# The MLP's features of groups 1 to 3 as seven products of half-size blocks

## The chip, the cores and the metric

The kernel runs on one core of one Trainium2 chip. Its metric is the device time of one execution in microseconds (us); a median over runs is given. Five engines work side by side, each through its own instructions in order: TensorE (PE in the profile; its weight loads are PEld), VectorE (DVE), ScalarE (ACT), GpSimd (POOL) and SyncE (SP, which here only issues DMAs).

## The reference, cut to what matters

A bidirectional encoder trunk of two layers on 512 tokens of width 1024. Layer 0 mixes tokens by a gated DeltaNet, layer 1 by GLA; behind each mixer stands a squared-ReLU MLP with a hidden width of 4096. The change lies in the MLP, which runs twice:

```python
def _sq_relu_mlp(h, w1, w2):
    a = jax.nn.relu(jnp.matmul(h, w1))       # w1: 1024 x 4096
    return jnp.matmul(a * a, w2)             # w2: 4096 x 1024
...
x = _layernorm(DEEPNORM_ALPHA * x + _sq_relu_mlp(x, mlp_w1[i], mlp_w2[i]), ln2_g[i], ln2_b[i])
```

Everything is float32.

## The kernel before

**Arithmetic.** Each float32 operand of a product is split into a high part (ACT casts it to fp32r, `split`, line 98) and the rest (VectorE subtracts, line 99). `mm3` (lines 117 to 119) then makes three matmuls: high by high, high by low, low by high. "A split" below is the pair of instructions of lines 98 and 99; on VectorE both of its inputs lie in SBUF.

**Groups.** `mlp` cuts the hidden width into G = 4 groups of GF = 8 features of 128 columns. A feature (`feature`, `proj_cm`) is W1's 128 columns times all of x, transposed (`xth`, `xtl`: 8 blocks of 128 rows, 512 tokens): 8 blocks x 3 matmuls, 24 matmuls of 512 columns into a PSUM bank `pj`; ACT then takes ReLU and square into `h` (`act`).

**W2 of groups 0 to 2.** `second` multiplies a group's activations by its rows of W2 as 2 x 2 blocks, in seven products instead of eight (Strassen's scheme in Winograd's form). The blocks of W2 are loaded by DMAs that POOL issues (`load_part`, line 371) into tiles `w2r`; the sums of blocks that the scheme needs are made by `plus` (line 390): DMAs that add one tile to another, issued by POOL. The differences of activations are made by VectorE (`s1`, `a21`, `a11`, `a12`). A product has 24 matmuls of 512 columns, into banks X, Y, Z; VectorE adds the result to the residual `xt` (`add`, lines 406 and 408).

**Order.** Group 0's first four features run in two halves of 256 tokens (`proj_halves`), the rest plainly. Then each product of group gi is followed by one feature of group gi + 1 (`nxt`): seven products, eight features. Group 3's W2 (`last`) is multiplied plainly, by token tiles (banks `pl`), with a LayerNorm behind each tile. The order on PE and POOL is that of the text (`in_order`); ACT and VectorE are ordered by the scheduler of the framework, when the kernel is compiled. Tiles come from rings by tag: `wst` (W1 as loaded, 3), `wh`/`wl` (3), `w2r` (10), `w2h`/`w2l` (3), `ah`/`al` (2).

In the second MLP, `affine` applies the previous LayerNorm's scale and shift to x on VectorE in group 0 (lines 201 and 202).

Of the kernel before, what the change touches and what calls it, by code (L numbers as in the profile page):

```python
# [28 lines left out]
class Ctx:  # L29
# [153 lines left out]
    def whiten(self, xs):  # L183

        nc = self.nc
        st = self.small.tile([P, 2, 6], F32, name="bst", tag="bst1", bufs=4)
# [48 lines left out]
    def layernorm(self, z, out, par, last=False, split=1):  # L235
# [3 lines left out]
        st = self.small.tile([P, 2 * split, 6], F32, name="bst", tag=f"bst{split}", bufs=4 // split)  # L239
# [91 lines left out]
def mlp(c, w1, w2, g, b, left, before=None, out=None):  # L331
# [13 lines left out]
    with c.banks(pj=2, X=2, Y=2, Z=2), tc.tile_pool(name="mlp", bufs=2) as pool:  # L345
        par = None
        acts = []
# [3 lines left out]
        RING = {"ah": ("ah", "al", 2), "w2": ("w2h", "w2l", 3), "raw": ("w2r", "w2r", 10)}  # L351
# [9 lines left out]
        def raw():  # L361
            return pool.tile([P, 2, 512], F32, name="w2r", tag="w2r", bufs=10)
# [24 lines left out]
        def plus(a, b):  # L387

            for q in range(2):
                nc.gpsimd.dma_start(blocks[a + (q,)], blocks[b + (q,)], accum_op=ALU.add)  # L390

# [3 lines left out]
        def feature(gi, f, h):  # L395
            return act(c.proj_cm(w1, (gi * GF + f) * P, "pj"), h[f // HF][:, f % HF, :])
# [12 lines left out]

        def quarters(h):  # L410
            return [h[j][:, :, HT * i:HT * i + HT] for i in range(2) for j in range(2)]

        def second(gi, h, a, nxt):

            a11, a12, a21, a22 = quarters(h)
# [4 lines left out]
            def product(bk, a, i, new, by_tile=False):  # L420

                if i not in parts:
                    split(i)
                ws = parts.pop(i)
                order = [(q, j) for j in range(2) for q in range(2)] if by_tile else [(q, j) for q in range(2) for j in range(2)]
                for q, j in order:
                    wh, wl = ws[q]
                    sl = slice(j * P, (j + 1) * P)
                    for k in (2 * q, 2 * q + 1):
                        c.mm3(bk[j], a[0][:, k, sl], a[1][:, k, sl], wh[:, k % 2, :], wl[:, k % 2, :],  # L430
                              new and k == 0, k == HF - 1, skip_group_check=True)

            def fetch(i, j):
                if gi + 2 < G:
                    load(gi + 1, i, j, acts[-1])

            X, Y = banks("X"), banks("Y")
            product(X, a, 1, True)
            for j in range(2):
                add(j, 0, X[j])  # L440
            nxt()
            Z = banks("Z")
            product(Z, pair(a12), 2, True)
            s1 = pool.tile([P, HF, HT], F32, name="s1", tag="s1", bufs=1)
            V.tensor_tensor(s1, a22, a21, ALU.subtract)
            V.tensor_tensor(a21, a11, a21, ALU.subtract)
# [1129 lines left out]
```

## Time and profile before

| | |
|---|---|
| Median of 3 runs (lowest, highest) | 1369.61 us (1368.17, 1369.61) |
| The profiled execution: its time, its span | 1368.45 us, 1366.5 us |
| Mean TensorE clock granted | 0.996 of full speed |
| Busy in the span: PE, DVE, ACT, POOL | 98%, 70%, 51%, 10% |
| First MLP: first product of W2, first matmul of group 3's W2 | 475.56 us, 721.8 us |
| Mean DMA rate | 104 GB/s |

How to read it: the span goes from the first to the last instruction; the time of an execution also holds what lies around it. Times of instructions are microseconds from the span's start, then the duration. Matmuls overlap, so that what one costs in a row of them is the distance from start to start, not its duration. In rows of groups, "x" is the count, then come the busy time and the mean length in ns, and after the bar the idle time of the engine before these instructions and what ended it. The idle time of an engine that is not the bottleneck costs nothing.

### The profile page before, as it was taken

To read this page: it belongs to the slowest core of one execution; us is meant where nothing else is said; L and a number is where in the kernel's file an instruction comes from. 1 tells how busy PE (TensorE), PEld (TensorE's weight loads), DVE (VectorE), ACT (ScalarE), POOL (GpSimd) and SP (SyncE) were. 2 spreads that over 40 slices of the span, in tenths; PEclk is the share of its full clock that TensorE was granted. 3 is DMA by queue.
4 is the path that set the end of the run, shared out by engine and by line. 5 is a ranking of instruction groups with operands and counts; after the bars stand their busy time and mean duration, and the time that the engine had idled before them with its cause. 6 is when DMAs were issued, how large, how long until landed. Compare 5 with 4: busy or idle time off the path is not lost.

```text
span 1366.5 us, 20078 instructions
## 1 busy us (share of the span) xinstructions
PE 1345.9 (98%) x7925; PEld 1114.8 (82%) x7925; DVE 950.7 (70%) x1502; ACT 692.7 (51%) x1293; POOL 138.0 (10%) x216
## 2 busy tenths in 40 slices
PE   7999999999999999999999999999999999999997
PEld 6778787877788888888888988888879888888886
DVE  5798988888867375655655677977773956556555
ACT  3667566565734554444443354654466544444430
POOL 6000040000002111201000000000001212120000
PEclk9999999999999999999999999999999999999999
DMA  6311121211234676747522222221224957566121
GB/s 166 88 48 47 38 57 47 63 48 32 79 96 121 190 167 196 172 124 185 108 93 59 62 84 77 62 63 62 90 65 150 228 148 214 139 191 133 50 81 55
DMA packets 148261, 142.62 MB, mean 104 GB/s; under 512 B 9583, under 2 KB 124391, under 8 KB 148167
## 3 DMA queue, kind: packets, MB, share of 16 engines
q1 hardware_dynamic: 132224, 86.45, 22.2%
q0 software_dynamic: 15232, 54.55, 15.9%
q8 instruction: 62, 1.02, 0.3%
q10 hardware_dynamic: 711, 0.34, 0.1%
q14 instruction: 32, 0.26, 0.1%
HBM read 114.06 MB, written 2.10 MB: 85 GB/s over the span
## 4 chain that ended last, share of the span: by engine, by line
PE 89%; ACT 5%; DVE 2%; POOL 1%; issue 1%; DMA 1%; SPq 0%; DVEq 0%; POOLq 0%; ACTq 0%
PE pj L118 8%; PE pj L117 8%; PE pj L119 8%; PE pjv L118 3%; PE pjv L119 3%; PE pjv L117 3%; PE pX L119 2%; PE pX L117 2%; PE pX L118 2%; PE pl L117 2%; PE pl L119 2%; PE pl L118 2%; PE scp L817 2%; PE op L1506 2%; PE lv L1382 2%; PE pZ L119 2%
## 5 line engine op out<-in xcount | busy, mean ns | idle before, releaser
L99 DVE TENSOR_TENSOR wl<-wst,wh 128x1024 fp32r<-128x1024 f32 x137 | 169.3, 1237 | 186.8 <-ACT wh L98 186.8
L98 ACT CAST wh<-wst 128x1024 fp32r<-128x1024 f32 x137 | 144.0, 1051 | 250.1 <-PE pj L118 182.1
L118 PE MATMUL pj<-xtl,wh 128*128 128x512 f32 (+1 forms) x544 | 202.1, 371 | 0.3 <-DVE xtl L168 0.3
L117 PE MATMUL pj<-xth,wh 128*128 128x512 f32 (+1 forms) x544 | 202.1, 371 | 0.3 <-ACT xth L167 0.3
L119 PE MATMUL pj<-xth,wl 128*128 128x512 f32 (+1 forms) x544 | 201.7, 371 | 0.0
L99 DVE TENSOR_TENSOR w2l<-w2r,w2h 128x1024 fp32r<-128x1024 f32 x84 | 102.5, 1221 | 62.8 <-ACT w2h L98 62.7
L118 PEld LDWEIGHTS pj<-xtl,wh 128*128 128x128 f32 x544 | 102.5, 188 | 18.5 <-DVE xtl L168 0.8
L117 PEld LDWEIGHTS pj<-xth,wh 128*128 128x128 f32 x544 | 102.4, 188 | 18.4 <-ACT xth L167 0.5
L119 PEld LDWEIGHTS pj<-xth,wl 128*128 128x128 f32 x544 | 102.5, 188 | 17.7
L98 ACT CAST w2h<-w2r 128x1024 fp32r<-128x1024 f32 x84 | 88.3, 1052 | 44.9 <-PE pZ L119 14.4
L98 ACT CAST ah<-h 128x1024 fp32r<-128x1024 f32 x40 | 42.1, 1052 | 41.6 <-PE pX L118 16.9
L371 POOL DMA_DIRECT2D w2r<-in_mlp_w x48 | 35.0, 731 | 276.0 <-ACT h L358 178.5
L390 POOL DMA_DIRECT2D w2r<-w2r x48 | 41.4, 926 | 178.9 <-DVE w2l L99 123.5
L117 PE MATMUL pX<-w2h,ah 128*128 128x512 f32 x144 | 56.3, 391 | 0.0
L119 PE MATMUL pX<-w2h,al 128*128 128x512 f32 x144 | 56.3, 391 | 0.0
L118 PE MATMUL pX<-w2l,ah 128*128 128x512 f32 x144 | 56.0, 389 | 0.0
L99 DVE TENSOR_TENSOR al<-h,ah 128x1024 fp32r<-128x1024 f32 x40 | 48.9, 1222 | 9.6 <-ACT ah L98 8.1
L117 PE MATMUL pjv<-wh,xth 128*128 128x512 f32 x128 | 54.7, 427 | 0.0
L119 PE MATMUL pjv<-wh,xtl 128*128 128x512 f32 x128 | 50.2, 392 | 0.0
L118 PE MATMUL pjv<-wl,xth 128*128 128x512 f32 x128 | 49.9, 390 | 0.0
L214 ACT ACTIVATE rsy<-rsv 128x1 f32<-128x1 f32 (+1 forms) x28 | 5.7, 203 | 77.9 <-DVE rsv L211 77.2
L117 PE MATMUL pjk<-xth,wh 128*128 128x512 f32 (+1 forms) x112 | 42.3, 378 | 0.3 <-ACT wh L98 0.3
(440 smaller groups left out, 3460.2 us busy)
## 6 DMA issues: line engine op xcount, KB each, us to landing
wst<-in_mlp_w SPq DMA_DIRECT2D x80, 512.0 KB, 4.3
w2r<-in_mlp_w POOLq DMA_DIRECT2D x48, 512.0 KB, 5.7
w2r<-w2r POOLq DMA_DIRECT2D x48, 512.0 KB, 5.8
wst<-in_a_w_in SPq DMA_DIRECT2D x32, 512.0 KB, 4.1
wst<-in_b_w_in SPq DMA_DIRECT2D x32, 256.0 KB, 3.1
wst<-in_a_w_out SPq DMA_DIRECT2D x8, 512.0 KB, 3.9
wst<-in_b_w_in SPq DMA_DIRECT2D x8, 512.0 KB, 3.8
wst<-in_b_w_out SPq DMA_DIRECT2D x8, 512.0 KB, 3.6
```

The costliest lines, as they stand in the source:

```text
L98: nc.scalar.copy(hi, src)
L99: nc.vector.tensor_tensor(lo, src, hi.bitcast(F32), ALU.subtract)
L117: mm(ps, ah, bh, start=start, stop=False, **kw)
L118: mm(ps, ah, bl, start=False, stop=False, **kw)
L119: mm(ps, al, bh, start=False, stop=stop, **kw)
L214: nc.scalar.activation(y, v, AF.Ln, scale=-2.0)
L371: ins = nc.gpsimd.dma_start(t, w2[r:r + 2 * P, 512 * j:512 * j + 512].rearrange("(k p) n -> p k n", p=P))
L390: nc.gpsimd.dma_start(blocks[a + (q,)], blocks[b + (q,)], accum_op=ALU.add)
L817: T.matmul(ps[:, n, :], kh[:, sl], qh[:, sl], start=True, stop=True)
L1382: T.matmul(ps[:, u, :, :], lhs[:, u, :], cols(rhs, u, s, i), start=True, stop=True)
L1506: T.matmul(op[:, n, :], l, r, start=i == 0, stop=i == len(mm) - 1)
```

## The change

Pairs of features of groups 1 to 3 (12 pairs an MLP) become 2 x 2 block products: x in halves of 512 rows and of 256 tokens, W1 in halves of 512 rows and two features. Seven products of 4 blocks x 3 matmuls of 256 columns replace 2 x 24 matmuls of 512. The combinations of x are made once (`combos`, VectorE, in group 0, into tiles `t0` to `t5`, the last one in place of x's block). The sums of W1 blocks are GpSimd additions on the loaded tiles (`total`, four of 512 columns a pair), and the sums of W2 blocks become GpSimd additions too (`sums`, eight of 1024 columns a group) in place of DMAs. A pair has 3.5 splits of 1024 columns where it had two. The seven results are put together by ACT (copies out of PSUM) and VectorE (`pairs`).

W1's pairs (`pairs`) and W2's products (`seconds`, cut into units of six matmuls) are two generators; the main loop draws a step of one and a unit of the other in turn, seven of each for a pair. The order on ACT is now the written one, too, in this stretch. A product's splits are issued one product ahead, its additions to `xt` one unit behind. Five splits of group 3's W2 and activations are drawn into the last two products (`last`, now a generator with homes chosen by hand). Half of `affine` goes to GpSimd. The ring of `w2r` has 8 tiles instead of 10, the pool `small` 3 instead of 4.

The diff, cut:

```diff
-    def proj_cm(self, w, c0, tag, n=P, name="pj"):
-
-        wh, wl = self.wcols(w, c0, n)
+    def proj_cm(self, w, c0, tag, n=P, name="pj", parts=None):
+
+        wh, wl = parts or self.wcols(w, c0, n)
...
-            self.nc.vector.tensor_tensor(x, x, par[q], ALU.mult)
-            self.nc.vector.tensor_tensor(x, x, par[2 + q], ALU.add)
+            eng = self.nc.vector if q else self.nc.gpsimd
+            eng.tensor_tensor(x, x, par[q], ALU.mult)
+            eng.tensor_tensor(x, x, par[2 + q], ALU.add)
...
-        def split(i):
-
-            i_, j_ = {1: (0, 0), 2: (1, 0), 3: (1, 1), 4: (1, 0), 5: (0, 0), 6: (0, 0), 7: (0, 1)}[i]
-            parts[i] = [c.split(blocks[i_, j_, q], [P, 2, 512], pool=ring("w2")) for q in range(2)]
-
-            if i == 1:
-                plus((0, 0), (0, 1))
-                plus((0, 1), (1, 1))
-            elif i == 5:
-                plus((0, 0), (1, 1))
-                plus((1, 0), (0, 0))
-
-        def plus(a, b):
-
-            for q in range(2):
-                nc.gpsimd.dma_start(blocks[a + (q,)], blocks[b + (q,)], accum_op=ALU.add)
...
+        def combos():
+
+            f = lambda t: t.bitcast(F32)
+            tmp = pool.tile([P, 2, HF, HT], F32, name="tx", tag="h", bufs=3)
+            u, v = tmp[:, 0], tmp[:, 1]
+            a12, a21, a22 = x_block(0, 1), x_block(1, 0), x_block(1, 1)
+            op = {1: x_block(0, 0), 2: a12, 4: a22}
+
+            def pair_of(i, src, dst):
+                A.copy(dst[0], src)
+                V.tensor_tensor(dst[1], src, f(dst[0]), ALU.subtract)
+                op[i] = dst
+
+            def diff(out, a, b):
+                V.tensor_tensor(out, f(a[0]), f(b[0]), ALU.subtract)
+                V.tensor_tensor(out, out, f(a[1]), ALU.add)
+                V.tensor_tensor(out, out, f(b[1]), ALU.subtract)
+
+            def neg(out, a, b):
+                V.scalar_tensor_tensor(out, a, -1.0, f(b[0]), ALU.mult, ALU.subtract)
+                V.tensor_tensor(out, out, f(b[1]), ALU.subtract)
+
+            diff(v, a22, a21)
+            yield op
+            pair_of(5, v, t_pair(0))
+            yield op
+            diff(u, op[1], a21)
+            yield op
+            neg(v, u, a22)
+            yield op
+            pair_of(6, v, t_pair(1))
+            yield op
+            if before:
+                for t in range(NT):
+                    c.affine(t, lnp)
+                    yield op
+            neg(v, v, a12)
+            yield op
+            pair_of(3, v, t_pair(2))
+            yield op
+            while not_done:
+                yield op
+            pair_of(7, u, a21)
...
+        def pairs(op, hs):
+
+            raws, ws = {}, {}
+            N = (G - 1) * GF // 2
+            K = HF
+
+            def load1(n, i):
+                if n < N:
+                    raws[n, i] = t = c.wst.tile([P, KT, P], F32, name="wst", tag="wst")
+                    c.dma(t, w1[:, (GF + 2 * n + i) * P:(GF + 2 * n + i + 1) * P].rearrange("(k p) n -> p k n", p=P))
+
+            def total(a, b):
+                nc.gpsimd.tensor_tensor(a, a, b, ALU.add)
+
+            def half(n, i, k):
+                return raws[n, i][:, K * k:K * k + K, :]
+
+            def halves(i, j, t):
+                ws[i], ws[j] = [[x[:, K * k:K * k + K, :] for x in t] for k in range(2)]
+
+            def first(n):
+                if n < N:
+                    halves(1, 2, c.split(raws[n, 0], [P, KT, P]))
+                    total(half(n, 0, 0), half(n, 1, 0))
+
+            def second_(n):
+                if n < N:
+                    ws[5] = c.split(half(n, 0, 0), [P, K, P])
+                    total(half(n, 0, 0), half(n, 1, 1))
+                    total(half(n, 0, 1), half(n, 0, 0))
+                    total(half(n, 1, 0), half(n, 1, 1))
+
+            def prod(i, ps, new):
+                (wh, wl), (xh, xl) = ws[i], op[i]
+                for k in range(K):
+                    c.mm3(ps, wh[:, k, :], wl[:, k, :], xh[:, k, :], xl[:, k, :], new and k == 0, k == K - 1, skip_group_check=True)
+
+            def bank():
+                return c.bank([P, S], F32, name="pq", tag="pj")[:, :HT]
+
+            load1(0, 0)
+            load1(0, 1)
+            first(0)
+            second_(0)
+            load1(1, 0)
+            yield
+            for n in range(N):
+                gi, f = 1 + n // (GF // 2), 2 * n % GF
+                if f == 0:
+                    hs[gi] = new_h()
+                h = hs[gi]
+                h1, h2 = [h[(f + i) // HF][:, (f + i) % HF, :] for i in range(2)]
+                t1, t2 = slice(0, HT), slice(HT, S)
+                X = bank()
+                prod(1, X, True)
+                A.copy(h1[:, t1], X)
+                Z = bank()
+                prod(2, Z, True)
+                V.tensor_tensor(h1[:, t1], h1[:, t1], Z, ALU.add)
+                halves(6, 4, c.split(raws[n, 0], [P, KT, P]))
+                load1(n + 2, 0)
+                yield
+                halves(7, 3, c.split(raws[n, 1], [P, KT, P]))
+                load1(n + 1, 1)
+                yield
+                Y = bank()
+                prod(5, Y, True)
+                A.copy(h2[:, t2], Y)
+                prod(6, X, False)
+                A.copy(h2[:, t1], X)
+                yield
+                first(n + 1)
+                yield
+                prod(7, X, False)
+                V.scalar_tensor_tensor(h2[:, t2], X, -1.0, h2[:, t2], ALU.mult, ALU.subtract)
+                prod(3, Y, False)
+                V.scalar_tensor_tensor(h2[:, t1], h2[:, t1], -1.0, Y, ALU.mult, ALU.subtract)
+                second_(n + 1)
+                yield
+                prod(4, X, False)
+                A.activation(h1[:, t2], X, AF.Relu)
+                yield
+                act(h2, h2)
+                A.activation(h1[:, t1], h1[:, t1], AF.Relu)
+                acts.append(A.activation(h1, h1, AF.Square))
...
+        BLOCK = {1: (0, 0), 2: (1, 0), 3: (1, 1), 4: (1, 0), 5: (0, 0), 6: (0, 0), 7: (0, 1)}
+        PLUS = {1: (((0, 0), (0, 1)), ((0, 1), (1, 1))), 5: (((0, 0), (1, 1)), ((1, 0), (0, 0)))}
+
+        def split_q(gi, i, q):
+
+            parts.setdefault((gi, i), []).append(c.split(blocks[BLOCK[i] + (q,)], [P, 2, 512], pool=ring("w2")))
+            if (gi, i) != (0, 1):
+                sums(i, q)
+            if i in (6, 7, 3, 4):
+                load_part(gi + 1, *BLOCK[i], q)
+
+        def sums(i, q):
+
+            for x, y in PLUS.get(i, ()):
+                nc.gpsimd.tensor_tensor(blocks[x + (q,)], blocks[x + (q,)], blocks[y + (q,)], ALU.add)
...
+        def seconds(hs, tail):
+
+            seq = [(gi, i) for gi in range(G - 1) for i in (1, 2, 5, 6, 7, 3, 4)]
+            left = {}
+
+            def operand(gi, i):
+                a11, a12, a21, a22 = quarters(hs[gi])
+                if i == 5:
+                    V.tensor_tensor(a11, a11, a21, ALU.subtract)
+                    V.tensor_tensor(a21, a22, a21, ALU.subtract)
+                if i == 6:
+                    V.scalar_tensor_tensor(a21, a11, -1.0, a22, ALU.mult, ALU.subtract)
+                    V.scalar_tensor_tensor(a12, a12, -1.0, a21, ALU.mult, ALU.subtract)
+                left[gi, i] = pair({1: a11, 2: a12, 5: a21, 6: a21, 7: a11, 3: a12, 4: a22}[i])
...
+            for q in range(2):
+                split_q(0, 1, q)
+            operand(0, 1)
+            yield
+            due = []
+            for m, (gi, i) in enumerate(seq):
+                nx = seq[m + 1] if m + 1 < len(seq) else None
+                if i == 1:
+                    X, Y = banks("X"), banks("Y")
+                if i in (2, 4):
+                    Z = banks("Z")
+                bk = {1: X, 6: X, 7: X, 5: Y, 3: Y}.get(i) or Z
+                for u in range(4):
+                    q, j = divmod(u, 2)
+                    wh, wl = parts[gi, i][q]
+                    ah, al = left[gi, i]
                     sl = slice(j * P, (j + 1) * P)
                     for k in (2 * q, 2 * q + 1):
+                        c.mm3(bk[j], ah[:, k, sl], al[:, k, sl], wh[:, k % 2, :], wl[:, k % 2, :],
+                              i in (1, 2, 4, 5) and k == 0, k == HF - 1, skip_group_check=True)
+                    for d in due:
+                        adds(*d)
+                    due = [(i, j, bk[j])] if q else []
+                    if i == 6 and u == 2:
+                        adds(*due.pop())
+                    if m == 0 and u < 2:
+                        sums(1, u)
+                    if nx:
+                        if u in (0, 2):
+                            split_q(*nx, u // 2)
+                        elif u == 1:
+                            operand(*nx)
+                    if m >= len(seq) - 2:
+                        next(tail, None)
+                    yield
+            for d in due:
+                adds(*d)
...
+            weights(0, 0, 0, "wst", "wst")
+            yield
+            weights(0, 1, 0, "wst", "w2r")
+            yield
+            acts_of(0, 0)
+            yield
+            weights(0, 0, 1, "wh", "wl")
+            yield
+            weights(0, 1, 1, "w2r", "w2h")
+            yield
+            acts_of(0, 1)
+            weights(1, 0, 0, "w2l", "w2r")
+            weights(1, 1, 0, "w2h", "w2l")
+            weights(1, 0, 1, "w2r", "wh")
+            weights(1, 1, 1, "w2h", "wl")
+            acts_of(1, 0, "w2l", "w2r")
+            acts_of(1, 1, "w2r", "wh")
...
+            combo = combos()
+            def run(n):
+                for _ in range(n):
+                    next(combo, None)
+            op = next(combo)
+            run(3)
+            w = c.wcols(w1, GF // 2 * P)
             for f in range(4, GF):
+                nw = c.wcols(w1, (f + 1) * P) if f + 1 < GF else None
+                run(2)
+                done = feature(f, h, w)
+                w = nw
                 if f in (4, 5):
                     load_part(0, 1, 1, f % 2, done)
                 if f == 5:
                     load(0, 1, 0, acts[-1])
                 if f == 6:
+                    next(units)
+            work = pairs(op, hs)
+            next(work)
+            not_done.clear()
+            for _ in combo:
+                pass
+            with c.in_order(mybir.EngineType.Activation):
+                for _ in work:
+                    next(units)
+                next(units, None)
+            par.extend(c.load_ln(g, b, ln_tile(), acts[-1]))
+            for _ in tail:
+                pass
...
-        c = Ctx(tc, nc, (pool("const", 1), pool("big", 1), pool("wst", 3), pool("whl", 3), pool("small", 4)))
+        c = Ctx(tc, nc, (pool("const", 1), pool("big", 1), pool("wst", 3), pool("whl", 3), pool("small", 3)))
```

More of the change, by code (lines that the diff above doesn't have):

```diff
@@ L417, in banks, with adds @@
             def banks(tag):
                 return [c.bank([P, 512], F32, name="p" + tag, tag=tag) for _ in range(2)]
[L420 to L427, printed above, removed]
+            def adds(i, j, ps):
+                if i in (1, 2):
+                    add(j, 0, ps)
+                elif i in (5, 7):
+                    add(2 + j, 1, ps, ALU.subtract)
+                else:
+                    add(j, 1, ps, ALU.subtract) if i in (6, 3) else add(2 + j, 0, ps)
+                if i == 7:
+                    add(2 + j, 0, ps)
@@ L441, in second @@
[L441 to L446, printed above, removed]
-            V.scalar_tensor_tensor(a11, s1, -1.0, a11, ALU.mult, ALU.subtract)
-            for j in range(2):
-                add(j, 0, Z[j])
-            nxt()
-            product(Y, pair(s1), 5, True)
-            for j in range(2):
-                add(2 + j, 1, Y[j], ALU.subtract)
@@ L562, in mlp @@
-            for gi in range(G - 1):
-                more = gi + 2 < G
-                nh = new_h()
-                todo = iter(range(GF))
-                def nxt():
-                    f = next(todo)
-                    feature(gi + 1, f, nh)
-                    if f == 6 and more:
-                        load(gi + 1, 1, 0)
-                        split(1)
-                        nxt.a = pair(quarters(nh)[0])
-                second(gi, h, a, nxt)
-                if par is None:
-                    par = c.load_ln(g, b, lambda i: pool.tile([P, 512], F32, name=f"ln{i}", tag=f"ln{i}", bufs=1), acts[-1])
-                h, a = nh, nxt.a if more else None
```

162 lines of the change are left out of this document (70 added, 92 removed).

## Prediction

> **What bounds the kernel now.** I read the page's head first, for the engine that fills the span, and then one stage: the stretch of the first MLP that the change rewrites, from its first W2 product (475.56 us) to the start of the last group (721.4 us), in the view of windows.
>
> ```profile
> span 1366.5 us, 20078 instructions
> PE 1345.9 (98%) x7925; PEld 1114.8 (82%) x7925; DVE 950.7 (70%) x1502; ACT 692.7 (51%) x1293; POOL 138.0 (10%) x216
> 475.56:721.40 245.84, 245.84 (x1080) 202.49 (x1079) 148.40 (x149) 118.41 (x137) 32.74 (x42) 1.00 0.59 149
> ```
>
> The columns of the last row are length, busy time (and count) of PE, weight loads, DVE, ACT, POOL, then clock, DMA share and GB/s. TensorE never stops in this stretch: 1080 matmuls in 245.84 us, 0.2276 us each, at full clock. 504 of them are the 21 W2 products (24 each), 576 the 24 W1 features (24 each). DVE has 148.4 us of work, POOL 32.7 us, nearly all of it issuing DMAs. I call this stretch the core; the second MLP has one of the same make. TensorE's own work sets its length, so fewer TensorE columns shorten it if nothing else becomes longer than TensorE.
>
> **TensorE, removed and added.** Two neighbouring features (48 matmuls of 512 columns) become seven products of four blocks and three matmuls, 84 matmuls of 256 columns. What a matmul costs is its start-to-start distance, since durations overlap. First and last of one feature's 24 (the second row is the next product's first), then the first and the twenty-fifth of 25 matmuls of 256 columns, where the stage's opening runs them:
>
> ```profile
> 470.11 0.39 PE L117 MATMUL pj<-xth,wh 128*128 128x512 f32 x1
> 475.56 0.39 PE L117 MATMUL pX<-w2h,ah 128*128 128x512 f32 x1
> 442.32 0.28 PE L117 MATMUL pj<-xth,wh 128*128 128x256 f32 x1
> 445.19 0.28 PE L117 MATMUL pj<-xth,wh 128*128 128x256 f32 x1
> ```
>
> 5.45/24 = 0.227 us and 2.87/24 = 0.1196 us: half the columns cost 53%, not 50%. A pair of features goes from 48 x 0.227 = 10.90 us to 84 x 0.1196 = 10.05 us. With 12 pairs the core's TensorE work falls to 504 x 0.2276 + 12 x 10.05 = 114.7 + 120.6 = 235.3 us, 10.5 us less; two MLPs, 21 us. A seventh product saved is worth 12.5% on paper and 7.8% here, because of the narrower matmuls.
>
> The Trainium skill, page "TensorE: Matmul & The Clock Gate", section "Back-to-back issue gap", gives N/2.4 + 2.5 ns for a warm matmul: 109 and 216 ns. By that a pair would save 48 x 0.216 - 84 x 0.109 = 1.2 us and both MLPs 29 us; the rows above disagree (120 and 227 ns), and I go by the rows.
>
> **VectorE and GpSimd, added.** The block sums of W2 leave the DMA queues and those of W1 are new; both become GpSimd additions of two SBUF operands. VectorE gets wider weight splits (3.5 tiles a pair for 2) and combines products. What such instructions do to each other is seen at the kernel's beginning, on POOL and DVE, and once more before the first MLP:
>
> ```profile
> 14.01 1.26 POOL L1016 TENSOR_TENSOR off<-blk 128x512 f16<-128x512 f32 x1
> 15.21 0.34 POOL L1005 MEMSET blk<- 128x128 f32 x2
> 16.81 3.50 POOL L1016 TENSOR_TENSOR off<-blk 128x512 f16<-128x512 f32 x2
> 14.79 0.69 DVE L168 TENSOR_TENSOR xtl<-tp,xth 128x512 fp32r<-128x512 f32 x1 [0.16 <-ACT xth L167]
> 16.90 2.28 DVE L99 TENSOR_TENSOR wl<-wst,wh 128x1024 fp32r<-128x1024 f32 x1 [0.23 <-ACT wh L98]
> 19.29 2.10 DVE L99 TENSOR_TENSOR wl<-wst,wh 128x1024 fp32r<-128x1024 f32 x1
> 427.65 1.22 DVE L99 TENSOR_TENSOR wl<-wst,wh 128x1024 fp32r<-128x1024 f32 x1
> 427.68 2.35 POOL L253 TENSOR_TENSOR xt<-xt,lnp 128x512 f32<-128x512 f32 x1 [3.59 <-ACT xt L252]
> 435.05 1.28 POOL L253 TENSOR_TENSOR xt<-xt,lnp 128x512 f32<-128x512 f32 x1 [5.03 <-ACT xt L252]
> 503.97 1.23 DVE L99 TENSOR_TENSOR al<-h,ah 128x1024 fp32r<-128x1024 f32 x1
> 505.12 1.22 DVE L99 TENSOR_TENSOR w2l<-w2r,w2h 128x1024 fp32r<-128x1024 f32 x1
> 524.52 0.68 DVE L408 TENSOR_TENSOR xt<-xt,pX 128x512 f32<-128x512 f32 x1
> 525.12 0.68 DVE L406 SCALAR_TENSOR_TENSOR xt<-xt,pX 128x512 f32<-128x512 f32 x1
> ```
>
> A split alone takes 1.22 us (pitch 505.12 - 503.97 = 1.15), a GpSimd addition of 512 columns alone 1.28 (pitch 15.21 - 14.01 = 1.20). Met by the other, each is stretched by the other's length: the split to 2.28 and 2.10, the addition to 2.35. Two additions and two splits between 16.81 and 21.39 us took 4.58 us, which is the sum of the four and not the longer pair. So they exclude each other, in both directions. The split of 14.79 us, one of whose inputs is a PSUM bank, ran inside the addition of 14.01 us at its usual 0.69: with one SBUF input there is no exclusion.
>
> The Trainium skill, "SBUF — State Buffer", section "Who interferes with whom", says the same as a rule: a VectorE instruction with two SBUF inputs and a GpSimd instruction that reads SBUF share a read port, and the second to start is fully blocked. Without that rule the sum would stop at TensorE's 235.3 us a core and come to about 1348 us; with it, to the forecast below. The 4.58 us agree with it.
>
> **The shared time of one core, counted.** VectorE, two SBUF inputs, 1024 columns: W1 splits 35 (three a pair, one fewer at the end); W2 weight halves 40; activation splits 20 and one of the x combinations; activation differences 12; tail splits drawn into the last two products 5. That is 113 x 1.15 = 130.0 us, and 11 half-width splits at 0.60, 6.6: together 136.6. GpSimd: 44 W1 additions of 512 columns at 1.15 (4.58/2 less a split's 1.15), 50.6 us, and 24 W2 additions of 1024. No row shows that width on POOL; bounds are the 1.28 us above and twice that, 2.56. The 128-column addition below gives a slope: (1.28 - 0.46)/384 = 2.1 ns a column, so 1.15 + 512 x 0.0021 = 2.25 us, 54 us in all. GpSimd 104.6; both 241.
>
> ```profile
> L611 POOL TENSOR_TENSOR fo<-fo x6: 450/461/474, 181.6 to 188.2; 128x128 f32<-128x128 f32 x6
> L842 DVE TENSOR_TENSOR E<-E,F 128x256 f32<-128x256 f32 x56 | 21.6, 417 | 2.1 <-POOL E L802 1.1 <-ACT F L739 0.8
> ```
>
> VectorE also has work with one SBUF input: 48 additions of W2 products at 0.60 (525.12 - 524.52), 28.8 us, and 36 feature combinations of 256 columns at about 0.34 (417 ns less the 0.08 by which neighbours overlap), 12.2: 41 us, 178 us of VectorE work in all. These may run beside a GpSimd addition, but VectorE takes its instructions in order, and one that waits for the port holds back everything behind it.
>
> So a core lasts at least 241 us (port always taken) and at most 178 + 104.6 = 282 us (no overlap at all), against 245.84 now. Between the ends I let the 41 us fall at random: GpSimd holds the port for 105 us of some 265, so 0.39 of 41, 16 us, are covered, and the core takes 282 - 16 = 266 us. That is 20 us more, 40 us in two MLPs. I take no idle time of both for granted, and no better luck.
>
> **What is late next.** TensorE, with 235 us, waits for VectorE at: the W1 splits (products 6 and 7), the step in which product 4 writes the bank that the combination of product 7 must first have read (cover: product 3, 12 x 0.1196 = 1.44 us, and a unit of six W2 matmuls, 1.37 us), and the W2 banks. A second loop is the W1 chain: split for product 5 (ACT and DVE, 0.6 each), three GpSimd additions (3.5 us, up to 1.15 more each when a split is ahead), cast and split for product 6 (1.05 + 1.15): 7 to 11 us, behind it all later GpSimd additions. Its cover, from the buffer that product 3 or 4 frees to product 6 of the next pair, is 9.8 to 12.6 us of TensorE work. I cost it at nothing, covered by those matmuls; without that cover it adds up to 1.1 us a pair, 13 us a core (rival 3).
>
> **Smaller parts.** (a) The x combinations: 14 VectorE instructions of 1024 columns, 16 us, in the opening of the MLP, eight of them before the split of feature 4:
>
> ```profile
> 447.50:470.00 22.50, 22.50 (x127) 19.73 (x126) 6.20 (x6) 11.00 (x15) 5.01 (x8) 1.00 0.60 182
> 442.94 0.69 DVE L168 TENSOR_TENSOR xtl<-tp,xth 128x512 fp32r<-128x512 f32 x1
> 446.35 1.23 DVE L99 TENSOR_TENSOR wl<-wst,wh 128x1024 fp32r<-128x1024 f32 x1 [1.09 <-ACT wh L98]
> 453.78 0.40 PE L117 MATMUL pj<-xth,wh 128*128 128x512 f32 x1
> ```
>
> VectorE has 16.3 of those 22.5 us free, so the work fits. But x is complete at 443.6 us and eight instructions last until 452.8; if the split of feature 4 (now 446.35) stands behind them it ends at 454.0, and TensorE starts that feature at 453.78. 0 to 1.3 us an MLP (one split more in front); I take 0.5. (b) The W2 sums by DMA go:
>
> ```profile
> L390 POOL DMA_DIRECT2D w2r<-w2r x48 | 41.4, 926 | 178.9 <-DVE w2l L99 123.5 <-DMA w2r<-w2r 47.3 <-issue 8.0
> L371 POOL DMA_DIRECT2D w2r<-in_mlp_w x48: 714/724/770, 436.6 to 1210.1; - x48
> ```
>
> 24 issues a core at 0.93 us, hidden before, so no gain; each load of W2 (0.72, never stretched, so it takes no port) still waits on POOL for the split that frees its block, and the additions queue behind it: inside the spread. (c) ACT gains 11 casts, 11 half casts and some 50 small copies, about 40 us on 118.41: 160 of 235, covered; in written order a cast that waits for a GpSimd sum holds up the W2 casts behind it. (d) SP still loads 24 W1 tiles a core. (e) Half of `affine` (8 additions, 9 us of port) goes to POOL in the second MLP's opening, ahead of W2 loads on its queue; not needed before the first addition to x. (f) One small buffer fewer in all stages: 0 to about 5 us (28 normalisations at 0.2), taken as 0. (g) The tail begins with 7 splits instead of 12 after the core; TensorE did not stop there before, so no gain.
>
> **The sum.** The profiled execution took 1368.45 us (span 1366.5 and 1.95 around it), 1.2 below the median of the runs. 1368.45 + 2 x (266 - 245.8) + 2 x 0.5 = 1410 us.
>
> **Rivals.** (1) The overlap is good enough and TensorE still sets the pace: 1368.45 - 21 + 1 = 1348. For it: the port's 241 us are near 235.3, its hold may be some per cent under the pitch I used, and rings of three let work be drawn ahead. Against: it needs the port taken 98% of the time and nearly all of the 41 us covered. It decides where VectorE and GpSimd together fit in 245.8 us, which is 36 of 41 us overlapped: above that the change is a gain. (2) A wash, the two sides cancelling near that point: within 2.7 us of 1369 (0.2%, about what a measurement of this kernel tells from no change). (3) No overlap, and the W1 chain on top: 282 to 295 us a core, 1368.45 + 2 x 36.2 + 1 = 1442 and, at 295, 1468. For it: written order on three engines, each waiting in turn; against: VectorE's additions come in groups of two to four (0.60 apart), beside which GpSimd can run.
>
> **How the numbers follow.** Forecast (core 253 to 277, 1384 to 1432) 0.48; (1) 0.25; (2) 0.05; (3) 0.22. Faster 0.25, same 0.05, slower 0.70. The range goes down to 1347, to keep most of (1), and up to 1444, where half of (3) begins; about 0.2 is outside. The forecast's own range is 1384 to 1432.
>
> **What would show it.** Right: in the core TensorE with gaps that end at DVE `wl` and `w2l` splits or at DVE reads of the `pq` banks; 256-column matmuls 0.12 us apart; many L99 splits above 1.3 us and POOL additions of 512 columns well above 1.28; a core of about 266 us. Wrong, if splits keep their 1.22 us beside POOL additions, or if TensorE runs through without gaps in about 235 us: then work was drawn ahead far enough to let the port be taken nearly always. Wrong the other way, if the chain of W1 sums (POOL waits for DVE, ACT waits for POOL) stands ahead of most gaps.

## The result, and the profile after

The changed kernel takes 1460.32 us (median of 5 runs, 1456.02 to 1462.41) against 1369.49 us before: ratio 1.0663, 95% interval 1.0643 to 1.0682. The forecast was 1410 us, at most 1444: the direction was right, the size was not. The page of the changed kernel, its head and the row of the granted clock in tenths (before: 9 in every slice):

```profile
span 1460.7 us, 22147 instructions
PE 1360.9 (93%) x8789; PEld 1164.0 (80%) x8789; DVE 1187.7 (81%) x1642; ACT 755.5 (52%) x1445; POOL 429.4 (29%) x336
PEclk9999999999999999899999999999998898998999
```

TensorE lost five points of its share, POOL went from 138 to 429 us, and the clock row has 8s. The first core and the second MLP's, from the first W1 product to the first matmul of group 3's W2, in the view of windows (columns as in the prediction):

```profile
476.00:761.20 285.20, 250.18 (x1513) 225.17 (x1512) 243.15 (x204) 145.32 (x208) 165.89 (x94) 0.93 0.28 84
1110.10:1408.50 298.40, 254.94 (x1513) 228.41 (x1512) 253.21 (x214) 148.25 (x211) 172.88 (x96) 0.91 0.27 82
```

They last 285.2 and 298.4 us (before: 245.8 and 245.9). Together they are 92 us longer, nearly all of the 94 us by which the span grew. In the first, TensorE is busy for 250.2 us and idle for 35. What VectorE and GpSimd took for their instructions there (view of groups by shape):

```profile
L99 DVE TENSOR_TENSOR w2l<-w2r,w2h 128x1024 fp32r<-128x1024 f32 x40 | 66.9, 1672 | 10.5 <-ACT w2h L98 10.4
L99 DVE TENSOR_TENSOR wl<-wst,wh 128x1024 fp32r<-128x1024 f32 x35 | 63.8, 1829 | 4.0 <-ACT wh L98 4.0
L99 DVE TENSOR_TENSOR al<-h,ah 128x1024 fp32r<-128x1024 f32 x20 | 34.4, 1722 | 5.2 <-ACT ah L98 5.2
L444 POOL TENSOR_TENSOR wst<-wst 128x512 f32<-128x512 f32 x46 | 79.5, 1738 | 56.3 <-DVE wl L99 36.3 <-DVE h L508 8.0 <-DVE h L506 6.4
L552 POOL TENSOR_TENSOR w2r<-w2r 128x1024 f32<-128x1024 f32 x24 | 71.2, 2968 | 4.4 <-DVE w2l L99 3.5
```

A split takes 1.7 to 1.8 us on average for 1.22, an addition of 512 columns 1.74 for 1.28. (Line 444 adds W1's blocks, line 552 W2's.) One of the long waits, seen on POOL, DVE and PE (view of instructions in order of time):

```profile
563.92 5.22 POOL L552 TENSOR_TENSOR w2r<-w2r 128x1024 f32<-128x1024 f32 x2
569.09 6.72 POOL L444 TENSOR_TENSOR wst<-wst 128x512 f32<-128x512 f32 x3
575.78 5.62 POOL L552 TENSOR_TENSOR w2r<-w2r 128x1024 f32<-128x1024 f32 x2
...
566.79 3.43 DVE L99 TENSOR_TENSOR al<-h,ah 128x1024 fp32r<-128x1024 f32 x1
570.26 2.20 DVE L562 TENSOR_TENSOR h<-h 128x1024 f32<-128x1024 f32 x1
572.38 2.30 DVE L99 TENSOR_TENSOR w2l<-w2r,w2h 128x1024 fp32r<-128x1024 f32 x1
574.60 1.27 DVE L529 TENSOR_TENSOR xt<-xt,pZ 128x512 f32<-128x512 f32 x2
575.79 3.40 DVE L563 TENSOR_TENSOR h<-h 128x1024 f32<-128x1024 f32 x1
579.12 3.35 DVE L99 TENSOR_TENSOR wl<-wst,wh 128x1024 fp32r<-128x1024 f32 x1
582.40 0.41 DVE L490 TENSOR_TENSOR h<-h,pq 128x256 f32<-128x256 f32 x1
...
572.89 0.39 PE L119 MATMUL pX<-w2h,al 128*128 128x512 f32 x1
582.86 0.58 PE L117 MATMUL pq<-t,wh 128*128 128x256 f32 x1 [9.59 <-DVE h L490]
583.24 0.42 PE L118 MATMUL pq<-t,wh 128*128 128x256 f32 x1
```

Seven GpSimd additions and five VectorE instructions with two SBUF inputs go in turns, each stretched by the other: VectorE's five take 14.7 us, where five at 1.22 us would take some 6. The two additions into `xt`, which read PSUM, pass at their usual pace (574.60). TensorE wants a bank for product 5. Product 2's result still lies in it; line 490, 0.41 us long, reads it out, but it stands on VectorE behind all of these. The wait is 9.59 us. All waits of the W1 products in both cores (view of one tile, `pq`, and what ended the idle time before it):

```profile
  DVE h L490: 64.1, 12
  DVE h L506: 6.6, 3
  DVE wl L99: 5.7, 3
  ACT h L358: 2.0, 1
```

And what follows this wait: the matmul of 583.24 us starts 0.38 us after the first, the later ones 0.21 us apart instead of 0.12. The window behind the wait (clock in the third column from the end):

```profile
582.86:587.00 4.14, 4.14 (x19) 4.14 (x20) 3.35 (x3) 0.37 (x1) 0.00 (x0) 0.50 0.54 149
```

The granted clock is half. In the two cores TensorE has twelve waits of 3.5 us or more (the longest 9.8), and the record of the granted clock has twelve stretches at half, one with each of them. The Trainium skill, "TensorE: Matmul & The Clock Gate", section "Part 1: The HAM clock gate", names these two states, half and full, and about 3.4 us of sustained work to come back. The trace agrees on the states; coming back took 4.8 us here (the pitch is 0.12 again from 587.7 us).

### The profile page after: what moved, and what is told of

It reads as the page before. It is cut to its first block, busy times and chain, and to the rows that moved or that the text cites. A ratio compares the mean times of both kernels' runs of the same rounds, so it can differ in the third digit from the quotient of the medians.

```text
span 1460.7 us, 22147 instructions
## 1 busy us (share of the span) xinstructions
PE 1360.9 (93%) x8789; PEld 1164.0 (80%) x8789; DVE 1187.7 (81%) x1642; ACT 755.5 (52%) x1445; POOL 429.4 (29%) x336
## 4 chain that ended last, share of the span: by engine, by line
PE 70%; DVE 15%; ACT 6%; issue 4%; DMA 3%; POOL 2%; SPq 0%; DVEq 0%; POOLq 0%; ACTq 0%
PE pq L117 4%; PE pq L119 4%; PE pq L118 4%; DVE wl L99 3%; PE pjv L118 3%; PE pjv L117 3%; PE pjv L119 3%; DVE w2l L99 3%; DVE al L99 3%; PE pl L118 2%; PE pl L117 2%; PE pl L119 2%; PE scp L989 2%; DMA wst<-in_mlp_w 2%; PE op L1678 2%
## 5 line engine op out<-in xcount | busy, mean ns | idle before, releaser
L99 DVE TENSOR_TENSOR wl<-wst,wh 128x1024 fp32r<-128x1024 f32 (+1 forms) x179 | 255.4, 1430 | 65.0 <-ACT wh L98 64.9
L98 ACT CAST wh<-wst 128x1024 fp32r<-128x1024 f32 (+1 forms) x179 | 177.4, 993 | 202.6 <-POOL wst L444 105.7
L444 POOL TENSOR_TENSOR wst<-wst 128x512 f32<-128x512 f32 x96 | 167.2, 1752 | 120.9 <-DVE wl L99 85.4
L117 PE MATMUL pq<-t,wh 128*128 128x256 f32 x288 | 92.3, 321 | 64.1 <-DVE h L490 64.1
L552 POOL TENSOR_TENSOR w2r<-w2r 128x1024 f32<-128x1024 f32 x48 | 142.4, 2968 | 8.8 <-DVE w2l L99 7.0
L117 PEld LDWEIGHTS pq<-t,wh 128*128 128x128 f32 x288 | 64.2, 223 | 69.8 <-DVE h L490 69.4
L117 PE MATMUL pq<-xth,wh 128*128 128x256 f32 x384 | 110.5, 288 | 8.6 <-DVE h L506 6.6
L119 PE MATMUL pq<-xth,wl 128*128 128x256 f32 x384 | 110.5, 288 | 5.7 <-DVE wl L99 5.7
L118 PE MATMUL pq<-xtl,wh 128*128 128x256 f32 x384 | 109.9, 286 | 0.0
L119 PE MATMUL pq<-t,wl 128*128 128x256 f32 x288 | 90.9, 316 | 0.0
L118 PE MATMUL pq<-t,wh 128*128 128x256 f32 x288 | 90.2, 313 | 0.0
L99 DVE TENSOR_TENSOR al<-h,ah 128x1024 fp32r<-128x1024 f32 x42 | 71.1, 1692 | 10.6 <-ACT ah L98 10.4
L118 PEld LDWEIGHTS pq<-t,wh 128*128 128x128 f32 x288 | 64.4, 224 | 0.4
```

The costliest lines, as they stand in the source:

```text
L98: nc.scalar.copy(hi, src)
L99: nc.vector.tensor_tensor(lo, src, hi.bitcast(F32), ALU.subtract)
L117: mm(ps, ah, bh, start=start, stop=False, **kw)
L118: mm(ps, ah, bl, start=False, stop=False, **kw)
L119: mm(ps, al, bh, start=False, stop=stop, **kw)
L444: nc.gpsimd.tensor_tensor(a, a, b, ALU.add)
```

## The experiments

The theories: A, VectorE and GpSimd exclude each other while both read SBUF, and that is the loss; B, the order the scheduler chose on VectorE is at fault; C, GpSimd is simply too slow a place for the sums. Edits are against the changed kernel unless said.

**The sums replaced by GpSimd work that reads nothing, and left out.**

```diff
 # e5_memsets
-nc.gpsimd.tensor_tensor(a, a, b, ALU.add)                      # W1; W2's sums alike
+[nc.gpsimd.memset(a, 0.5) for _ in range(2)]
 # e8_nosums
+pass
```

> Each GpSimd addition is replaced by two GpSimd memsets of the same tile (0.95 us each for 1024 columns in the profile of before), so that GpSimd has work of about the same length in the same places of its queue, which everyone waits for as before, but reads nothing from SBUF; the sums are left out of the computation. Theory A: no read, no exclusion; VectorE splits go back to 1.22 us and the time to 1345 to 1375 us. Theory B: order and waits unchanged, above 1430 us. Theory C: GpSimd as late as before, above 1430 us.

> All block sums of W1 and W2 are left out of the computation; everything else is as in the changed kernel. It bounds what the sums cost in all. Theory A and theory C: TensorE sets the pace, 1368 less 21 us, 1345 to 1360 us. Theory B: line 490 is late even so, and the time stays above 1400 us. The new widths alone (half of the columns at 53% of the time) would be wrong if it came out above 1360 us without gaps on TensorE.

Memsets: 1358.51 us, ratio 0.9930 (0.9915 to 0.9945). No sums: 1357.59 us, 0.9922 (0.9905 to 0.9938). With memsets, the groups of POOL and of VectorE's splits in the first core, and then the core's window:

```profile
L552 POOL MEMSET w2r<- 128x1024 f32 x48 | 45.1, 954 | 6.4 <-DVE w2l L99 5.0
L444 POOL MEMSET wst<- 128x512 f32 x89 | 45.4, 524 | 53.4 <-DVE wl L99 50.9
...
L99 DVE TENSOR_TENSOR w2l<-w2r,w2h 128x1024 fp32r<-128x1024 f32 x40 | 48.9, 1221 | 18.7 <-ACT w2h L98 18.3 <-PE pZ L119 0.3
L99 DVE TENSOR_TENSOR wl<-wst,wh 128x1024 fp32r<-128x1024 f32 x35 | 42.5, 1221 | 8.6 <-ACT wh L98 8.6
```

```profile
474.70:711.40 236.70, 236.70 (x1514) 215.48 (x1513) 178.06 (x204) 145.38 (x208) 107.25 (x161) 1.00 0.34 101
```

Without sums, the window of the same core:

```profile
474.90:711.50 236.60, 236.60 (x1513) 215.43 (x1512) 178.00 (x204) 145.21 (x208) 17.34 (x24) 1.00 0.34 101
```

GpSimd has 90 us of memsets in this core, against 107 that the additions would take alone by the prediction's prices (46 x 1.15 + 24 x 2.25), in the same places of its queue, and TensorE does not wait in it. VectorE's 204 instructions of this core stand in the same order in the traces of the changed kernel, of memsets and of no sums. So B and C fall as main causes: the same order and nearly the same GpSimd work cost nothing as long as GpSimd reads no SBUF. (A memset also does not wait for the second operand of the sum; the runs below that add on VectorE keep that wait.) The rows also give what VectorE's work is when nothing meets it: 178.0 us. In the changed kernel it was 243.2: 65 us of the first core are stretching, and VectorE still sat idle for 42.

**VectorE in the written order.**

```diff
-            with c.in_order(mybir.EngineType.Activation):
+            with c.in_order(mybir.EngineType.Activation), c.in_order(mybir.EngineType.DVE):
```

> The changed kernel with VectorE, too, held to the written order in the core; nothing else. Theory A: the same work on the shared port, 241 to 282 us a core, so 1420 to 1460 us. Theory B: line 490 comes ahead of the splits behind it, the long gaps before product 5 go (32.8 us of TensorE's waits in the first core), 1360 to 1390 us. Theory C: unchanged within 1%, 1445 to 1475 us.

1450.61 us, 1.0604 (1.0588 to 1.0620). Line 490's waits fell from 64 to 12 us, those at line 506 and at the W1 splits rose from 12 to 33. The order chooses where the loss shows and is worth 10 us of 91.

**The sums moved off GpSimd.**

```diff
 # e1: W2's sums
-nc.gpsimd.tensor_tensor(blocks[x + (q,)], blocks[x + (q,)], blocks[y + (q,)], ALU.add)
+nc.gpsimd.dma_start(blocks[x + (q,)], blocks[y + (q,)], accum_op=ALU.add)
 # e7: W2's sums;  e3: W1's and W2's;  e9: W1's as here, W2's as in e1
+V.tensor_tensor(...)
```

> The changed kernel with W2's block sums put back on DMAs; W1's sums stay GpSimd additions. Theory A (VectorE and GpSimd exclude each other, and the sum of their work is what a core lasts): GpSimd's 24 additions of 1024 columns, 54 us a core, leave the shared port, whose demand falls from 241 to 187 us; TensorE sets the pace again, 1350 to 1380 us. Theory B (the order that the scheduler chose on VectorE is at fault: the addition of product 2, line 490, which frees the bank for product 5, stands behind splits that wait for something else): the order is nearly kept, so the time stays above 1430 us. Theory C (GpSimd is just too slow a place in the chain of sums, port or not): the W1 chain with its four additions a pair stays, 1400 to 1430 us.

> The changed kernel with W2's sums as VectorE additions and W1's as GpSimd additions, as changed. Theory A: VectorE 178 + 27.6 = 206 us a core, GpSimd 51 us on the shared port; together 257 less what overlaps, so 240 to 257 us a core, 1360 to 1400 us, between the kernel with all sums on VectorE and the one with W2's sums by DMA (1422). Theory C: 1410 us or more.

> The changed kernel with all block sums, of W1 and W2, as VectorE additions; GpSimd adds nothing. Theory A (exclusion between VectorE and GpSimd): no partner, no exclusion; VectorE has 178 + 24 x 1.15 + 44 x 0.60 = 232 us of work a core beside TensorE's 235, so 1358 to 1390 us. Theory C (the chain of sums is what is slow, wherever it runs): the same chain, now behind more VectorE work, 1410 us or more.

> The changed kernel with W1's sums as VectorE additions and W2's by DMA, as before the change; GpSimd adds nothing. Theory A: VectorE 178 + 26.4 = 204 us a core, no exclusion: TensorE sets the pace, 1352 to 1368 us, a gain on both kernels. If the DMAs that add W2's tiles are what kept the kernel with W2's sums by DMA at 1422 us (POOL waited 69.7 us of the first core for such DMAs, with W1's additions queued behind), then W1's sums no longer stand behind them, and the same 1352 to 1368 follows; if those DMAs are late for W2's own products, 1380 us or more. Theory C: 1400 us or more.

| W1's sums | W2's sums | us | ratio (interval) |
|---|---|---|---|
| GpSimd | DMA | 1421.96 | 1.0398 (1.0376 to 1.0420) |
| GpSimd | VectorE | 1400.41 | 1.0230 (1.0215 to 1.0245) |
| VectorE | VectorE | 1395.01 | 1.0192 (1.0176 to 1.0207) |
| VectorE | DMA | 1372.34 | 1.0029 (1.0020 to 1.0039) |

Giving VectorE 54 us more work a core makes the kernel 65 us faster. All four came out above what A had said: the second row by less than 1 us, the other two on VectorE by 4 to 5, and the first by 42. The last row, where no W1 addition stands behind the DMAs on POOL's queue, is 50 us faster than the first, but it has no GpSimd additions either, so no run isolates what those DMAs cost. The first row's trace shows them wait for each other there (waits of POOL in its first core):

```profile
POOL w2r L552 <- DMA w2r<-w2r: 69.7, 12, 9.0
```

**One half of the change in the kernel before** (edit against the kernel before).

```diff
-nc.gpsimd.dma_start(blocks[a + (q,)], blocks[b + (q,)], accum_op=ALU.add)
+nc.gpsimd.tensor_tensor(blocks[a + (q,)], blocks[a + (q,)], blocks[b + (q,)], ALU.add)
```

> The kernel before, with W2's block sums as GpSimd additions in place of DMAs and nothing else of the change. Theory A: VectorE has 139 us of work a core and GpSimd 54 us on the shared port, 193 together, under TensorE's 246: no change, 1364 to 1374 us, with splits stretched and covered. A rival by which every stretched split costs TensorE time, however much slack there is: 24 additions x 1.1 us x 2, 50 us, about 1420 us.

1376.76 us, 1.0059 (1.0042 to 1.0075), 3 us above what A had said: splits average 1.42 to 1.50 us and are covered, but for one place, the second MLP's opening, where `affine` meets the first four additions (VectorE, POOL, TensorE in order of time):

```profile
1061.34 11.22 DVE L201 TENSOR_TENSOR xt<-xt,ln 128x512 f32<-128x512 f32 x2
1062.51 9.49 POOL L390 TENSOR_TENSOR w2r<-w2r 128x1024 f32<-128x1024 f32 x4
1080.97 0.80 PE L119 MATMUL pj<-xth,wl 128*128 128x512 f32 x1 [6.13 <-DVE wl L99]
```

The first row is two VectorE multiplications of 0.68 us: the first ran as usual, the second was held for 10 us, through four GpSimd additions. Here they did not take turns.

**Each half of the sums alone.**

```diff
 # h1: W2's sums left out      # h2: W1's sums left out
-nc.gpsimd.tensor_tensor(...)
+pass
```

> The changed kernel with W2's block sums left out of the computation; W1's stay GpSimd additions. Theory A in its plain form (a core lasts as long as the work that excludes each other): 178 us of VectorE and 51 of GpSimd are 229, under TensorE's 236.6, so nearly the time without any sums, 1358 to 1375 us. Theory D (the exclusion counts where it falls on a chain: GpSimd's four additions a pair, stretched by splits, lie between the split for product 5 and that for product 6, and TensorE waits for the end of that chain however free the port is on average): 1385 us or more.

> The changed kernel with W1's block sums left out of the computation; W2's stay GpSimd additions of 1024 columns. Theory A in its plain form: 178 and 54 us are 232, under 236.6: 1358 to 1378 us. Theory D: W2's sums are ready long before their products, they are on no chain, and only stretch splits: 1358 to 1385 us, clearly less than with W1's sums alone. If it comes out the slower of the two, it is the long additions (2.3 us, two in a row) that hold VectorE, and with it the addition that frees the bank for product 5.

W1's alone: 1372.88 us, 1.0034 (1.0022 to 1.0046). W2's alone: 1414.19 us, 1.0337 (1.0321 to 1.0352). Above the 1357.6 us without sums that is 15, 57 and, for both, 103. Theory A in its plain form fails for W2's: 178 + 54 = 232 us fit under TensorE's 236.6, and the first core took 262.8 (window):

```profile
474.90:737.70 262.80, 244.86 (x1514) 220.00 (x1513) 213.90 (x205) 145.42 (x208) 78.45 (x46) 0.97 0.30 91
```

VectorE is stretched by 36 us, which with its 178 would fit; but TensorE stood still for 18 and lost 8 more to the clock. Theory D, in the expectations above (only sums on a chain count), fails, too: those that lie on one, W1's, are the cheap ones.

**The long additions spread, or cut.**

```diff
 # i1 (all sums), i4 (W1's left out): two additions each behind products 1, 2, 5, 6
-PLUS = {1: (((0, 0), (0, 1)), ((0, 1), (1, 1))), 5: (((0, 0), (1, 1)), ((1, 0), (0, 0)))}
+PLUS = {1: (((0, 0), (0, 1)),), 2: (((0, 1), (1, 1)),), 5: (((0, 0), (1, 1)),), 6: (((1, 0), (0, 0)),)}
 # i2: each addition of 1024 columns as two of 512
+[nc.gpsimd.tensor_tensor(X[:, k, :], X[:, k, :], Y[:, k, :], ALU.add) for k in range(2)]
```

> As the kernel with W1's block sums left out of the computation (1414 us), with W2's GpSimd additions spread: two 1024-column additions behind each of the splits for products 1, 2, 5 and 6, instead of four behind 1 and four behind 5. The same work, the same widths. Burst theory (what counts is the port in the few us in which W2's additions come together and the addition of line 490 stands behind them, not the port's share of a core): the bursts are half as long, 1375 to 1400 us. Average theory (a core's total on the port): unchanged, 1408 to 1420 us.

> The changed kernel (1460 us), complete, with W2's GpSimd additions spread over the splits for products 1, 2, 5 and 6. Burst theory: 1415 to 1445 us. Average theory: 241 to 282 us a core as before, 1452 to 1468 us.

> The changed kernel, complete, with each GpSimd addition of 1024 columns cut into two of 512 columns, at the same place. Grain theory (each VectorE instruction that meets a GpSimd addition waits for the whole of it, so 1.15 us instead of 2.25, and VectorE gets in twice as often): 1425 to 1450 us. Burst and average theory (the work that excludes each other is the same): 1450 to 1468 us.

W2's alone, spread: 1405.39 us, 1.0273 (1.0259 to 1.0287), between the two expectations: line 490's waits fell from 28.2 to 9.3 us, those at line 506 rose from 1.9 to 17.3. Complete and spread: 1441.69 us, 1.0548 (1.0530 to 1.0567); halved: 1440.66 us, 1.0530 (1.0514 to 1.0546). So bursts and grain are worth about 19 and 20 us of 103, and neither is the whole.

**The second MLP's opening, and the place of product 4.**

```diff
 # f1: W1's sums on VectorE, W2's by DMA, and this; j1: this alone
-eng = self.nc.vector if q else self.nc.gpsimd
+eng = self.nc.vector
 # f2: as f1, VectorE in written order
 # i3: as f1, and this; j2: this alone
-                prod(4, X, False)
-                A.activation(h1[:, t2], X, AF.Relu)
                 yield
+                prod(4, X, False)
+                A.activation(h1[:, t2], X, AF.Relu)
                 act(h2, h2)
```

> No GpSimd arithmetic beside VectorE: W1's sums on VectorE, W2's by DMA, and the affine step of the second MLP all on VectorE, as before the change. Theory A: against the kernel with only the sums moved (1372 us) the gaps of 6.6 and 1.8 us at the beginning of the second core shrink: VectorE does 4.8 us more there and is not stopped for about 9; 1360 to 1368 us, a gain on the kernel before. If VectorE's own work in that opening is what is late, not the exclusion: 1370 to 1377 us.

> As the kernel beside it (W1's sums and affine on VectorE, W2's sums by DMA), with VectorE held to the written order in the core. If the order chosen by the scheduler is what leaves 9 us of waits for the combination behind product 7, they go: 5 to 9 us less than the kernel beside it, 1353 to 1362 us. If those waits come from VectorE's load at that place, no difference, or up to 10 us more because the written order puts splits behind each other that could run earlier.

> The kernel with W1's sums and affine on VectorE and W2's sums by DMA (1367 us), with product 4 of each pair moved one unit of six W2 matmuls later, so that VectorE has 1.37 us more to read product 7's bank before product 4 writes it. If TensorE's waits for that read (line 506, 7 us in the first core) and the half clock behind them are what is left of the gain: 1358 to 1364 us, faster than both kernels. If VectorE's load as a whole (204 of 237 us) is what is late, the wait moves to the next step: 1365 to 1370 us.

> The changed kernel with the affine step all on VectorE again, all block sums still on GpSimd. If the exclusion in the second MLP's opening (gaps of 1.2, 5.4 and 2.3 us and the half clock behind them) is its own part of the loss: 1448 to 1456 us. If VectorE is merely late there: 1457 us or more.

> The changed kernel with product 4 a unit later and all sums on GpSimd. If the place of product 4 were what made the faster version fast, 1440 us or less. By the exclusion it is not: the waits for line 490 (64 of 79 us that product matmuls of W1 wait for) stay, 1450 to 1462 us.

| | us | ratio (interval) |
|---|---|---|
| f1 | 1367.26 | 0.9995 (0.9986 to 1.0003) |
| f2 | 1388.96 | 1.0151 (1.0138 to 1.0164) |
| i3 | 1358.68 | 0.9931 (0.9917 to 0.9945) |
| j1 | 1456.01 | 1.0646 (1.0627 to 1.0664) |
| j2 | 1452.51 | 1.0620 (1.0602 to 1.0638) |

`affine` back on VectorE is worth 5 us where the rest is right; in the changed kernel it is about 4, where the single runs of the two overlap. The written order on VectorE costs 22 us here, where a gain or at most 10 us had been expected. Product 4 a unit later gains 8.6 us in the version without GpSimd additions (the waits at line 506 fall from 11.2 to 1.4 us) and 7.8 in the changed kernel, so it is not what makes up for the sums. The version with all of this, i3, is 0.7% faster than the kernel before. Its first core (window), and then the waits of its W1 products in both cores:

```profile
475.70:713.90 238.20, 237.44 (x1514) 215.06 (x1513) 202.53 (x248) 144.91 (x207) 37.18 (x47) 1.00 0.63 152
```

```profile
  ACT h L513: 2.6, 1
  DVE wl L99: 2.0, 2
  DVE h L506: 1.4, 4
```

238.2 us, with the full seven-product saving, full clock and VectorE at 202.5 of 238 us.

## Why the prediction was wrong

**Right.** The saving on TensorE: 235.3 us a core forecast, 236.6 measured without sums. VectorE's work: 178 forecast, 178.0 measured. That the exclusion makes the change a loss: shown by the memsets. The signs named: gaps that end at the read of a `pq` bank, matmuls of 256 columns at 0.12 us, splits and additions stretched. But the list of what is late next did not have the read that counted: 64 of the 78 us of waits end at line 490, which frees the bank for product 5, and 7 at the read behind product 7 that it named.

**The step that failed** is "so 0.39 of 41, 16 us, are covered, and the core takes 282 - 16 = 266 us", with its "I take no idle time of both for granted". The idle time, put at nothing, was 26 us a core. The cores took 285.2 and 298.4. In the first, VectorE was stretched by 65 us, so some 42 of GpSimd's 107 us ran while VectorE did something else or nothing: 26 beside its work, where 16 were forecast, and 16 while it was idle. One or the other computed in 259.4 us (the stretches of their instructions in the trace, overlaps counted once), less than the 266; but in the other 25.8 us neither did, and in the second core in 26.8. The trace shows a circle of waits: VectorE for ACT's casts, these for GpSimd's W1 sums (47 us in the first core), and those for VectorE's splits (36 us). VectorE's own idle time is the 16 and the 26, 42 us, and 178 + 65 + 42 is the 285. The sum over a core was the wrong measure in itself: W2's sums alone, 232 us of work for 236.6, cost 57 us (two cores and the openings). The additions come in bursts beside the one instruction that frees a bank. A smaller miss is the price of an addition of 1024 columns: in the kernel before with such sums four in a row took 9.49 us, 2.37 each and not 2.25, which makes 3 us a core.

**What the sum lacked.** The clock. TensorE's own 1512 matmuls took 250.2 us in place of 236.6, and 254.9 in the second core: 13.6 and 18.3 us more, at half clock behind waits, on top of 35 and 43.5 us of waiting. Each price of a wait has to be read with that. On TensorE the first core is 236.6 + 13.6 + 35.0; that is the same 285 as VectorE's sum above, counted on another engine, and nothing to add to it.

**What was costed at nothing and was not.** (e), half of `affine` on GpSimd: without any sums the second core still took 245.1 us for the first's 236.6, with one wait of 6.3 us for a W1 split in its beginning, and 2.2 us of half clock with it:

```profile
1059.00:1304.10 245.10, 238.78 (x1514) 216.76 (x1513) 188.69 (x213) 147.20 (x210) 19.49 (x26) 0.98 0.34 102
```

From e9 to f1, where only `affine` moves back, such waits of the second core fall from 6.4 to 2.0 us. (a), the combinations of x, cost nothing by themselves in the first MLP, where 0.5 us was forecast: without sums its core starts at 474.9 us, before the change at 475.6.

**The rivals.** Rival 3, no overlap and the W1 chain on top, 1442 to 1468 us, gives the time, but not for its reason, so that it came out is luck: 26 us of the first core did overlap, and with W1's sums alone the loss is 15 us. Rival 1, TensorE at 1348 us, is what the version i3 comes to within 11 us once GpSimd adds nothing. Still open is how the loss of 103 us divides: halves, spread and order each took 10 to 20 us of it, and waits that one of them removed came back in part at the next step. That the clock costs some 32 us, of which 2 stand in the kernel without sums, too, is read from TensorE's busy time and not tested by a run of its own.

## What to carry to other kernels

Before work goes from a DMA to GpSimd, look in the trace for a GpSimd instruction that reads SBUF beside a VectorE instruction with two SBUF inputs; if they stretch each other, count both as one engine, with bursts and not as a mean, and give VectorE the work if it has room (here 65 us faster than GpSimd, though still 37 behind no sums at all). Look for the short VectorE instruction that frees a PSUM bank and give it a product's distance: here one unit of six matmuls turned no change into a gain. Count more for a TensorE wait than its length: twelve of 3.5 to 9.8 us, 71 us in all, came here with half clock, which cost some 32 us more.

## What the runs showed of the hardware that was not expected

A VectorE instruction can be held through four GpSimd additions in a row (a multiplication of 0.68 us took 10.6), while elsewhere the two take turns one by one. As expected, 90 us of GpSimd memsets in the first core left its 75 VectorE weight splits of 1024 columns at 1.22 us and TensorE without a wait: writing alone does not collide, which the Trainium skill, "SBUF — State Buffer", section "Who interferes with whom", also states.
